# Four kinds of GpSimd products issued in pieces of 256 columns, in a two-block transformer kernel

## The chip, the cores and the metric

The kernel runs on 1 core of one Trainium2 chip. The metric is the device time of one execution in microseconds (us). Three runs of the kernel before took 1583.03, 1586.16 and 1586.99 us; their median, 1586.16 us, is the time before.

The names used below: PE is TensorE's matrix multiply, PEld its weight loads, DVE is VectorE, ACT is ScalarE, POOL is GpSimd, SP is SyncE, which issues the transfers.

## The reference, cut to what matters

Two layers of a first network (a pooling mixer, then stick-breaking attention, each followed by a gated addition) and two of a second one (latent attention, then differential attention, each with a layer norm) run on 512 tokens of 1024 features; the second network has 256 context tokens beside them.

```
h = rms_norm(x, a_norm);  x = x + pool_mixer(h, ...)           # layer 0
A[t,s] = beta[t,s] * prod_{s<j<t} (1 - beta[t,j])              # layer 1, stick-breaking
x = x + (o * silu(z)) @ b_w_out
x = x + (p[i] @ ple_w[i]) * sigmoid(x @ ple_gate_w[i])         # after each of both
x = layer_norm(ALPHA * x + gate * (o @ out_w[i]), ln_g, ln_b)  # second network, twice
```

Every weight matrix of the projections is multiplied with three fp32r products: a float32 number is split into a high part (rounded to fp32r) and a low part (the rest), and high·high, high·low and low·high are added.

## The kernel before, in words

The class `Block` writes the whole program: `layer0`, `layer1`, `mla`, `diff` (`build`, L1485). Activations lie with features or tokens on 128 partitions, 512 columns wide as a rule. A framework turns the calls into one list per engine and sets a semaphore wait wherever an instruction reads or overwrites what another wrote; regions of a tile are told apart, so that two instructions on different columns of one tile do not wait for each other.

**Weights.** `plan` lists units of up to 128x1024 numbers. `w()` hands out unit i and calls `w_advance` (L110): the transfer of unit i + 2 into one of three raw buffers, then the split of unit i + 1: ACT casts raw to the high part `wh` (L126), and L127 subtracts it from raw, which gives the low part `wl`. The first three units and two at the end have L127 on DVE, the other 159 on POOL. `fm` (L151) takes a unit as eight row blocks of 128 columns, `tm` (L157) as four of 256 columns; both walk through the row blocks in order, so the low part's columns are used from left to right, by the second or third product of each row block (L148, L149).

**Other POOL work of the four kinds.** `silu_mul` (L222) multiplies the gate of stick-breaking attention with its sigmoid (L225, 8 times 128x512). In `layer0`, `done` adds squares into `ssacc` (L500, 7 times 128x512). In `stick_steps` (L661), a step has three segments of 512, 384 and 128 columns, or two of 256: ACT makes sigmoid(-l) and sigmoid(l) (L707, L708), DVE scans each segment (L712, a product that runs backwards), POOL multiplies the weights `sb_b` with the scanned `sb_k`, one column further (L715: one instruction of 1023 columns, or two of 255), and PE transposes the result two steps later (`aT_p`, L172), from where ACT and DVE copy it (L731, L733).

**What POOL does besides, unchanged:** normalizing softmax rows (L1055, L1425), head norms (L528), rotary sums (L1000, L1353), and some sums of the layer norm (L818, L1163, L1179, L1180).

**The order of the work.** Each engine runs its list in order. `pipeline` (L254) sets the order inside the attention stages; elsewhere a list scheduler of the framework interleaves the calls.

DVE's part beside it: in the pooling mixer, sums over windows (L446, L449, L451), gates (L461, L463, L471), and the first product's scaling (L441), which frees a PSUM bank; in the layer norm of the second network, L1140 and L1141 (output rows), the small steps of `rsqrt` (L199 to L204), L1151, L1189 (which frees PSUM after the transposes `hT_p`) and the low parts of activations (L234).

Of the kernel before, what the change touches and what calls it, by code (L numbers as in the profile page):

```python
# [10 lines left out]
F32 = mybir.dt.float32  # L11
# [3 lines left out]
ALU = mybir.AluOpType  # L15
# [26 lines left out]
class Block:  # L42
# [67 lines left out]
    def w_advance(self, upto_dma, upto_split):  # L110
        nc = self.nc
        while self.w_dma < min(upto_dma, len(self.wq)):
            u = self.wq[self.w_dma]
            u["raw"] = self.wp.tile([P, 1024], F32, tag="wraw", name="wraw", bufs=3)
            for dst, src in u["src"](self._w_view(u["raw"], u["shape"])):
                nc.sync.dma_start(out=dst, in_=src)
            self.w_dma += 1
        while self.w_split < min(upto_split, len(self.wq)):
            i = self.w_split
            u = self.wq[i]  # L120
            n = math.prod(u["shape"])
            raw = u.pop("raw")
            pool, tag, size, bufs = u["own"] or ("weights", "", 1024, 4)
            h = self.pools[pool].tile([P, size], F32R, tag=tag + "wh", name="wh", bufs=bufs)
            l = self.pools[pool].tile([P, size], F32R, tag=tag + "wl", name="wl", bufs=bufs)
            nc.scalar.copy(h[:, :n], raw[:, :n])  # L126
            (nc.vector if i < 3 or pool == "ow3" else nc.gpsimd).tensor_tensor(out=l[:, :n], in0=raw[:, :n], in1=h[:, :n].bitcast(F32), op=ALU.subtract)  # L127
            u["hl"] = (self._w_view(h, u["shape"]), self._w_view(l, u["shape"]))
            self.w_split += 1

    def w(self):
        i = self.w_next
        self.w_next += 1
        self.w_advance(i + 3, i + 2)
        return self.wq[i].pop("hl")

    def w_cols(self, W, c0, n, own=None):
        return (lambda v: [(v, W[:, c0:c0 + n].rearrange("(k p) n -> p k n", p=P))], (W.shape[0] // P, n), own)
# [83 lines left out]
    def silu_mul(self, out, sg, z):  # L222

        self.nc.scalar.activation(sg, z, AF.Sigmoid)
        self.nc.gpsimd.tensor_tensor(out=out, in0=sg, in1=z, op=ALU.mult)  # L225

    def split(self, x, pool, tag, gain=None, n=512, bufs=8):

# [139 lines left out]
    def layer0(self):  # L368
        nc, a = self.nc, self.a
# [16 lines left out]
        for hf in range(2):  # L386
            for t in range(NT):
                cs = slice(hf * 512, hf * 512 + 512)
# [31 lines left out]
        pool = self.open("mix")  # L420
# [12 lines left out]
        for g, w in enumerate(POOL_WINDOWS):  # L433
# [32 lines left out]
            for j in range(2):  # L466
                c = 2 * g + j
# [7 lines left out]
        pool = self.open("ple0")  # L475
# [9 lines left out]
        pool = self.open("ple0b")  # L485
# [3 lines left out]
        ssacc = self.ssacc = self.sq_acc = xp.tile([P, 512], F32, name="ssacc")  # L489

        def done(c):
            x = xT[:, c, :]
            self.kv_acts.append(self.split(x, "kv", "kv", gain=self.v("kv_norm", c)))
            nc.sync.dma_start(out=self.xf[c], in_=x)
            if c == 0:
                nc.scalar.activation(ssacc, x, AF.Square)
            else:
                sq = pool.tile([P, 512], F32, tag="t2", name="sqc", bufs=4)
                nc.scalar.activation(sq, x, AF.Square)
                nc.gpsimd.tensor_tensor(out=ssacc, in0=ssacc, in1=sq, op=ALU.add)  # L500
            self.b_acts.append(self.split(x, "b", "b", gain=self.v("b_norm", c)))

        self.plan(self.l1_units())
# [157 lines left out]
    def stick_steps(self, c, ks, qs, vtok, ogs, pool):  # L661
# [31 lines left out]
        def first(n, segs):  # L693
            if n == 0 and c == 0:
                prep()
            Q, QL, K = h["Q"], h["QL"], h["K"]
            L = self.p_lg("sb_l")
            for e, i, o in segs:
                w = (i + 1) * P
                qi = slice(i * P, (i + 1) * P)  # L700
                nc.tensor.matmul(L[:, o:o + w], lhsT=Q[e][:, qi], rhs=K[e][:, :w], start=True, stop=False)
                nc.tensor.matmul(L[:, o:o + w], lhsT=QL[e][:, qi], rhs=K[e][:, :w], start=False, stop=False)
                nc.tensor.matmul(L[:, o + i * P:o + w], lhsT=self.identb, rhs=self.maskb, start=False, stop=True)
            kp = pool.tile([P, 1024], F32, tag="sb_k", name="sb_k", bufs=2)
            bt = h["bt", n] = pool.tile([P, 1024], F32, tag="sb_b", name="sb_b", bufs=4)
            vw = (lambda t: t) if len(segs) == 3 else (lambda t: t.rearrange("p (a b) -> p a b", b=512)[:, :, :256])
            nc.scalar.activation(vw(kp), vw(L), AF.Sigmoid, scale=-1.0)  # L707
            nc.scalar.activation(vw(bt), vw(L), AF.Sigmoid)  # L708
            for e, i, o in segs:
                w = (i + 1) * P  # L710
                rev = slice(o + w - 1, o - 1 if o else None, -1)
                nc.vector.tensor_tensor_scan(out=kp[:, rev], data0=kp[:, rev], data1=kp[:, rev], initial=1.0, op0=ALU.mult, op1=ALU.min)  # L712

            for o, w in ((0, 1024),) if len(segs) == 3 else ((0, 256), (512, 256)):
                nc.gpsimd.tensor_tensor(out=bt[:, o:o + w - 1], in0=bt[:, o:o + w - 1], in1=kp[:, o + 1:o + w], op=ALU.mult)  # L715
            if n == 1 and "next" in h:
                h["next"]()

# [800 lines left out]
```

## Time and profile before

| | |
|---|---|
| median of three runs | 1586.16 us |
| the profiled execution, its own time | 1584.99 us |
| its span, first to last instruction | 1583.2 us |
| PE busy / DVE busy / ACT busy / POOL busy | 1488.9 / 925.2 / 733.7 / 603.4 us |
| mean granted TensorE clock | 0.984 of full speed |

Busy times of engines overlap each other. A busy PE is not PE at its peak, because matmuls are pipelined and their ends are modelled. The time of an instruction that is held up by something other than a semaphore (a port that another engine has, for instance) counts as busy; the time before an instruction, while its semaphore is not there, counts as idle and is put down to the instruction that released it. An idle engine that is not the bottleneck costs nothing.

### The profile page before, as it was taken

The numbers are of one execution on the slowest core, as the hardware profiler recorded it, in microseconds if no ns is written. First come the engines' busy times: TensorE is split into PE (matmuls) and PEld (weight loads), VectorE is DVE, ScalarE is ACT, GpSimd is POOL, SyncE is SP. The second block draws the span as 40 slices with busy tenths as digits, with TensorE's granted clock in tenths as the row PEclk, the third lists the DMA queues.
The fourth block names the chain that finished last, engine by engine and source line by source line (L and its number), as shares of the span: only waits on it lengthen the run. The fifth ranks groups of instructions, "written<-read, shape, count | busy, mean of one in ns | idle before, by whom it ended". The sixth has DMA issues, their size and how long they took to land.

```text
span 1583.2 us, 24444 instructions
## 1 busy us (share of the span) xinstructions
PE 1488.9 (94%) x9590; PEld 1247.9 (79%) x9590; DVE 925.2 (58%) x1769; ACT 733.7 (46%) x1347; POOL 603.4 (38%) x431
## 2 busy tenths in 40 slices
PE   6999999999899899999999999997897999999997
PEld 4777889998555578888876667577797989999987
DVE  6676465532776656442465665547857655555576
ACT  5323344435666433332565555533335553555642
POOL 2533555643544453222333332444342424343310
PEclk9999999999999999999999999999899999999999
DMA  5323432323344334311103030434321112121122
GB/s 168 90 77 93 127 119 75 101 87 98 102 134 134 106 120 124 90 44 50 51 1 116 9 120 2 146 120 164 117 81 44 41 41 68 41 66 43 54 77 97
DMA packets 149747, 136.01 MB, mean 86 GB/s; under 512 B 12612, under 2 KB 135224, under 8 KB 149632
## 3 DMA queue, kind: packets, MB, share of 16 engines
q1 hardware_dynamic: 149632, 134.45, 27.4%
q8 instruction: 76, 1.25, 0.3%
q14 instruction: 39, 0.32, 0.1%
HBM read 126.02 MB, written 8.40 MB: 85 GB/s over the span
## 4 chain that ended last, share of the span: by engine, by line
PE 40%; DVE 7%; ACT 5%; issue 3%; DMA 2%; POOL 1%; SPq 0%; DVEq 0%; POOLq 0%; ACTq 0%
PE PT_p L172 4%; PE pv L1076 3%; PE qkv_p L147 2%; PE qkv_p L149 2%; PE qkv_p L148 2%; PE pv L1440 2%; PE gt_p L147 2%; PE gt_p L148 2%; PE gt_p L149 2%; PE lg L147 2%; PE lg L148 1%; ACT pe L1095 1%; PE lg L149 1%; DVE st L1094 1%; PE ada_p L787 1%
## 5 line engine op out<-in xcount | busy, mean ns | idle before, releaser
L127 POOL TENSOR_TENSOR wl<-wraw,wh 128x1024 fp32r<-128x1024 f32 (+2 forms) x159 | 377.0, 2380 | 377.9 <-ACT wh L126 364.8
L126 ACT CAST wh<-wraw 128x1024 fp32r<-128x1024 f32 (+2 forms) x164 | 166.3, 1020 | 282.1 <-issue 60.7
L1095 ACT ACTIVATE pe<-lg,st 128x768 f32<-128x768 f32 x160 | 130.5, 817 | 71.6 <-DVE st L1094 55.4
L1094 DVE TENSOR_REDUCE st<-lg 128x1 f32<-128x768 f32 x160 | 133.5, 843 | 38.8 <-PE lg L1421 20.1
L1055 POOL TENSOR_SCALAR pe<-pe,st 128x768 f32<-128x768 f32 (+1 forms) x96 | 73.4, 768 | 145.8 <-DVE st L1096 130.1
L147 PE MATMUL qkv_p<-wh,h 128*128 128x256 f32 x384 | 109.5, 285 | 0.9 <-ACT V L1366 0.7
L172 PE MATMUL PT_p<-ident,pe 128*128 128x128 f32 x640 | 99.6, 279 | 9.5 <-DVE pe L1426 3.3
L149 PE MATMUL qkv_p<-wh,h 128*128 128x256 f32 x384 | 108.1, 282 | 0.2 <-DVE h L234 0.2
L148 PE MATMUL qkv_p<-wl,h 128*128 128x256 f32 x384 | 108.1, 282 | 0.0
L172 PEld LDWEIGHTS PT_p<-ident,pe 128*128 128x128 f32 x640 | 72.6, 141 | 39.9 <-issue 16.9
L1425 POOL TENSOR_SCALAR pe<-pe,st 128x768 f32<-128x768 f32 x32 | 29.2, 912 | 126.7 <-DVE st L1424 85.5
L147 PE MATMUL out_p<-wh,o 128*128 128x256 f32 x256 | 74.5, 292 | 0.9 <-DVE y L1292 0.8
L147 PEld LDWEIGHTS qkv_p<-wh,h 128*128 128x128 f32 x384 | 72.5, 189 | 3.4 <-ACT V L1366 1.3
L148 PE MATMUL out_p<-wl,o 128*128 128x256 f32 x256 | 73.7, 290 | 1.4 <-POOL wl L127 1.4
L149 PE MATMUL out_p<-wh,o 128*128 128x256 f32 x256 | 73.5, 291 | 0.1
L147 PE MATMUL kv_p<-wh,kv 128*128 128x256 f32 x256 | 72.2, 282 | 1.2 <-ACT kv L236 1.2
L149 PEld LDWEIGHTS qkv_p<-wh,h 128*128 128x128 f32 x384 | 72.4, 189 | 0.4 <-DVE h L234 0.4
L148 PEld LDWEIGHTS qkv_p<-wl,h 128*128 128x128 f32 x384 | 72.6, 189 | 0.0
L148 PE MATMUL kv_p<-wl,kv 128*128 128x256 f32 x256 | 71.6, 280 | 0.0
L715 POOL TENSOR_TENSOR sb_b<-sb_b,sb_k 128x1023 f32<-128x1023 f32 (+1 forms) x32 | 43.0, 1355 | 74.2 <-DVE sb_k L712 44.9
L149 PE MATMUL kv_p<-wh,kv 128*128 128x256 f32 x256 | 71.2, 280 | 0.0
L712 DVE TENSOR_TENSOR_SCAN sb_k<-sb_k 128x512 f32<-128x512 f32 (+3 forms) x64 | 61.2, 996 | 10.4 <-ACT sb_k L707 10.3
(456 smaller groups left out, 4545.6 us busy)
## 6 DMA issues: line engine op xcount, KB each, us to landing
araw<-in_ada_w_dram SPq DMA_DIRECT2D x48, 512.0 KB
wraw<-in_diff_w_in_dram SPq DMA_DIRECT2D x32, 512.0 KB
wraw<-in_out_w_dram SPq DMA_DIRECT2D x24, 512.0 KB
wraw<-in_a_w_in_dram SPq DMA_DIRECT2D x16, 512.0 KB
wraw<-in_ple_gate_w_dram SPq DMA_DIRECT2D x16, 512.0 KB
wraw<-in_w_kv_dram SPq DMA_DIRECT2D x16, 512.0 KB
wraw<-in_b_w_in_dram SPq DMA_DIRECT2D x16, 512.0 KB
wraw<-in_mla_w_in_dram SPq DMA_DIRECT2D x11, 512.0 KB
```

Of the source, the lines that this page charges most:

```text
L126: nc.scalar.copy(h[:, :n], raw[:, :n])
L127: (nc.vector if i < 3 or pool == "ow3" else nc.gpsimd).tensor_tensor(out=l[:, :n], in0=raw[:, :n], in1=h[:, :n].bitcast(F32), op=ALU.subtract)
L147: mm(out, lhsT=lh, rhs=rh, start=start, stop=False)
L148: mm(out, lhsT=lh, rhs=rl, start=False, stop=False)
L149: mm(out, lhsT=ll, rhs=rh, start=False, stop=stop)
L172: self.nc.tensor.transpose(out, in_, self.ident[:in_.shape[0], :in_.shape[0]])
L712: nc.vector.tensor_tensor_scan(out=kp[:, rev], data0=kp[:, rev], data1=kp[:, rev], initial=1.0, op0=ALU.mult, op1=ALU.min)
L715: nc.gpsimd.tensor_tensor(out=bt[:, o:o + w - 1], in0=bt[:, o:o + w - 1], in1=kp[:, o + 1:o + w], op=ALU.mult)
L1055: nc.gpsimd.tensor_scalar(out=pe, in0=pe, scalar1=st[:, 1:2], scalar2=0.0, op0=ALU.mult, op1=ALU.add)
L1076: return nc.tensor.matmul(pv[64 * ee:64 * ee + 64, :], lhsT=V[:, k0 + k, vs], rhs=HH[px][:, k, :], start=(k == 0), stop=(k == nk - 1))
L1094: nc.vector.tensor_reduce(out=st[:, 0:1], in_=L, axis=AX.X, op=ALU.max, negate=True)
L1095: nc.scalar.activation(pe, L, AF.Exp, bias=st[:, 0:1], accum_out=st[:, 2:3])
```

## The change: the four kinds in pieces of 256 columns

A helper `pool_tt` issues a product of two tiles in pieces of 256 columns. L127 (where it is on POOL), L225, L500 and L715 go through it. No other line changes; what is computed is the same, element by element.

```diff
             nc.scalar.copy(h[:, :n], raw[:, :n])
-            (nc.vector if i < 3 or pool == "ow3" else nc.gpsimd).tensor_tensor(out=l[:, :n], in0=raw[:, :n], in1=h[:, :n].bitcast(F32), op=ALU.subtract)
+            if i < 3 or pool == "ow3":
+                nc.vector.tensor_tensor(out=l[:, :n], in0=raw[:, :n], in1=h[:, :n].bitcast(F32), op=ALU.subtract)
+            else:
+                self.pool_tt(l[:, :n], raw[:, :n], h[:, :n].bitcast(F32), ALU.subtract)
...
+    def pool_tt(self, out, in0, in1, op):
+
+        for c in range(0, out.shape[1], 256):
+            cs = slice(c, min(c + 256, out.shape[1]))
+            self.nc.gpsimd.tensor_tensor(out=out[:, cs], in0=in0[:, cs], in1=in1[:, cs], op=op)
...
-        self.nc.gpsimd.tensor_tensor(out=out, in0=sg, in1=z, op=ALU.mult)
+        self.pool_tt(out, sg, z, ALU.mult)
...
-                nc.gpsimd.tensor_tensor(out=ssacc, in0=ssacc, in1=sq, op=ALU.add)
+                self.pool_tt(ssacc, ssacc, sq, ALU.add)
...
-                nc.gpsimd.tensor_tensor(out=bt[:, o:o + w - 1], in0=bt[:, o:o + w - 1], in1=kp[:, o + 1:o + w], op=ALU.mult)
+                self.pool_tt(bt[:, o:o + w - 1], bt[:, o:o + w - 1], kp[:, o + 1:o + w], ALU.mult)
```

On POOL 206 instructions become 724: of L127 146 of 1024 columns, 4 of 768 and 9 of 512 become 614 of 256; of L715 16 of 1023 become 64, and 16 of 255 stay; of L225 and L500 15 of 512 become 30. The lists of DVE, ACT and SP keep their order row for row; PE's moves two tiny products of `ss1` by one row. What changes is POOL's list and who waits for what. In the changed file lines stand 3 to 12 further down; the helper's instruction is L144.

POOL in stick-breaking attention, before: two gates, two weight units and two steps' products (L715; 1023 columns for three segments, 255 for the two short ones). The brackets name the engines whose semaphores the instruction waits for.

```order
L715 TENSOR_TENSOR sb_b<-sb_b,sb_k 128x1023 [waits PE_49,DVE_49,Activation_49,Pool_49]
L225 TENSOR_TENSOR og<-sz,og 128x512 [waits Activation_49]
L127 TENSOR_TENSOR wl<-wraw,wh 128x1024 [waits DMAHW5_49,Activation_49]
L127 TENSOR_TENSOR wl<-wraw,wh 128x1024 [waits DMAHW0_49,Activation_49]
L715 TENSOR_TENSOR sb_b<-sb_b,sb_k 128x1023 [waits PE_49,DVE_49,Activation_49,Pool_49]
```

The same place in the changed kernel:

```order
L144 TENSOR_TENSOR sb_b<-sb_b,sb_k 128x255 [waits DVE_49]
L144 TENSOR_TENSOR og<-sz,og 128x256 [waits Activation_49]
L144 TENSOR_TENSOR og<-sz,og 128x256
L144 TENSOR_TENSOR wl<-wraw,wh 128x256 [waits DMAHW5_49,Activation_49]
L144 TENSOR_TENSOR wl<-wraw,wh 128x256 x3
L144 TENSOR_TENSOR wl<-wraw,wh 128x256 [waits DMAHW0_49,Activation_49]
L144 TENSOR_TENSOR wl<-wraw,wh 128x256 x3
L144 TENSOR_TENSOR sb_b<-sb_b,sb_k 128x256 [waits DVE_49,PE_49,Activation_49]
L144 TENSOR_TENSOR sb_b<-sb_b,sb_k 128x256 [waits DVE_49]
L144 TENSOR_TENSOR sb_b<-sb_b,sb_k 128x256
```

The pieces of a tile stand one behind the other where the tile stood. The first piece of a product waits for the first segment's scan, the second and the fourth for the next ones.

PE in the layer norm of the second network, before: four row blocks of a weight unit (L147 to L149; `out_p<-wl` takes the low part) with transposes of the next activations (`hT_p`) between them.

```order
L147 MATMUL out_p<-wh,o 128x256 [waits Activation_49]
L148 MATMUL out_p<-wl,o 128x256 [waits Pool_49]
L149 MATMUL out_p<-wh,o 128x256
L147 MATMUL out_p<-wh,o 128x256
L148 MATMUL out_p<-wl,o 128x256
L149 MATMUL out_p<-wh,o 128x256
L147 MATMUL out_p<-wh,o 128x256
L148 MATMUL out_p<-wl,o 128x256
```

The same place in the changed kernel:

```order
L156 MATMUL out_p<-wh,o 128x256 [waits Activation_49]
L157 MATMUL out_p<-wl,o 128x256 [waits Pool_49]
L158 MATMUL out_p<-wh,o 128x256
L156 MATMUL out_p<-wh,o 128x256
L157 MATMUL out_p<-wl,o 128x256 [waits Pool_49]
L158 MATMUL out_p<-wh,o 128x256
L156 MATMUL out_p<-wh,o 128x256
L157 MATMUL out_p<-wl,o 128x256 [waits Pool_49]
```

PE's products stand as they did; each row block now waits for its own quarter of the low part, the first one no longer for the whole tile.

## Rows read from the trace of the kernel before

**Rows 1.** Page, part 1: busy us, share of the span, instructions of each engine.

```profile
PE 1488.9 (94%) x9590; PEld 1247.9 (79%) x9590; DVE 925.2 (58%) x1769; ACT 733.7 (46%) x1347; POOL 603.4 (38%) x431
```

**Rows 2.** Busy us by stretch: length, PE, PEld, DVE, ACT, POOL, clock, DMA share, GB/s.

```profile
28.00:140.00 112.00, 99.77 (x413) 78.23 (x412) 82.29 (x95) 33.32 (x45) 49.77 (x27) 0.97 0.32 95
140.00:380.00 240.00, 238.05 (x1602) 217.26 (x1602) 108.78 (x170) 98.44 (x168) 124.79 (x64) 1.00 0.31 98
380.00:535.00 155.00, 141.04 (x809) 89.37 (x808) 112.59 (x164) 99.94 (x143) 73.92 (x48) 0.97 0.35 113
1050.00:1160.00 110.00, 92.26 (x715) 90.32 (x713) 79.83 (x170) 33.23 (x62) 51.32 (x23) 0.92 0.45 149
```

**Rows 3.** Waits of PE, whole span: us in total, times, longest us.

```profile
PE hT_p L172 <- DVE hm L1189: 12.3, 4, 5.8
PE u_p L147 <- DVE u L441: 5.9, 2, 4.3
PE z_p L147 <- DVE zr L461: 3.9, 2, 2.6
...
PE qT_p L172 <- DVE aT L733: 3.7, 1, 3.7
...
PE mix_p L147 <- DVE zr L471: 1.9, 2, 0.9
...
PE out_p L148 <- POOL wl L127: 1.4, 1, 1.4
```

**Rows 4.** Timeline, DVE then POOL, from 1101 us: start us, us, instruction, count.

```profile
1101.75 2.31 DVE L202 TENSOR_TENSOR rs_t<-rs_y,rs_m 128x1 f32<-128x1 f32 x1 [0.98 <-ACT rs_y L201]
1104.10 2.26 DVE L203 SCALAR_TENSOR_TENSOR rs_t<-rs_t,rs_y 128x1 f32<-128x1 f32 x1
1106.29 0.15 DVE L202 TENSOR_TENSOR rs_t<-rs_y,rs_m 128x1 f32<-128x1 f32 x1
...
1101.69 4.65 POOL L127 TENSOR_TENSOR wl<-wraw,wh 128x1024 fp32r<-128x1024 f32 x2 [4.14 <-ACT wh L126]
```

**Rows 5.** DVE groups by form: count | busy us, mean ns of one | idle us before.

```profile
L1141 DVE SCALAR_TENSOR_TENSOR y<-r,y 128x256 f32<-128x256 f32 x24 | 24.8, 1060 | 0.0
...
L463 DVE TENSOR_TENSOR sz<-sz,zr 128x512 f32<-128x512 f32 x8 | 17.1, 2143 | 4.4 <-ACT sz L462 4.4
...
L1140 DVE TENSOR_TENSOR y<-out_p,gate 128x256 f32<-128x256 f32 x24 | 9.2, 415 | 18.5 <-POOL gate L818 13.8 <-PE out_p L149 4.6
```

**Rows 6.** POOL groups by form.

```profile
L127 POOL TENSOR_TENSOR wl<-wraw,wh 128x1024 fp32r<-128x1024 f32 x146 | 357.3, 2456 | 331.4 <-ACT wh L126 324.9 <-issue 3.2 <-PE k_p L172 3.0
...
L715 POOL TENSOR_TENSOR sb_b<-sb_b,sb_k 128x1023 f32<-128x1023 f32 x16 | 32.4, 2022 | 60.1 <-DVE sb_k L712 43.5 <-ACT Q L687 8.3 <-PE aT_p L172 3.5
...
L1353 POOL TENSOR_TENSOR qr<-qr,rt 128x256 f32<-128x256 f32 x12 | 8.8, 738 | 7.2 <-DVE rt L1352 7.2
```

**Rows 7.** Timeline of the mixer's start, DVE, POOL, then PE.

```profile
28.93 2.94 DVE L446 TENSOR_TENSOR win<-u 128x527 f32<-128x527 f32 x1
31.91 1.64 DVE L449 SCALAR_TENSOR_TENSOR pl<-win,u 128x512 f32<-128x512 f32 x1
33.47 2.29 DVE L451 TENSOR_TENSOR hd<-win,invc 128x2 f32<-128x2 f32 x1
35.68 0.68 DVE L441 TENSOR_TENSOR u<-u_p,R 128x512 f32<-128x512 f32 x1
...
28.92 6.83 POOL L127 TENSOR_TENSOR wl<-wraw,wh 128x1024 fp32r<-128x1024 f32 x3 [3.34 <-ACT wh L126]
...
36.42 0.80 PE L147 MATMUL u_p<-h,wh 128*128 128x512 f32 x1 [4.32 <-DVE u L441]
```

**Rows 8.** Timeline of the layer norm, DVE.

```profile
1115.01 5.22 DVE L234 TENSOR_TENSOR hc<-hm,hc 128x256 fp32r<-128x256 f32 x3
```

**Rows 9.** Timeline of stick-breaking attention, DVE then POOL.

```profile
423.21 4.67 DVE L712 TENSOR_TENSOR_SCAN sb_k<-sb_k 128x256 f32<-128x256 f32 x2
...
419.53 5.47 POOL L127 TENSOR_TENSOR wl<-wraw,wh 128x1024 fp32r<-128x1024 f32 x2
424.96 3.95 POOL L715 TENSOR_TENSOR sb_b<-sb_b,sb_k 128x1023 f32<-128x1023 f32 x3
```

## The prediction

> **What bounds the kernel now.** I read the page first. PE is busy for 94% of the span, POOL for 38% [rows 1]: POOL is no bound by its sum, and what the change can give or take has to pass through a wait of PE. So I went to the stretches next. From 140 to 380 us PE is busy for 238 of 240 us; nothing that DVE or POOL does better there can shorten it. PE is short of work in the pooling mixer (12.2 of 112 us idle from 28 us), in stick-breaking attention (14.0 of 155 us from 380) and in the layer norm between the second network's layers (17.7 of 110 us from 1050) [rows 2]. Then PE's waits: the long ones there are for DVE, and all of them end when DVE has freed a PSUM bank: hT_p 12.3 us, u_p 5.9, z_p 3.9, qT_p 3.7, mix_p 1.9. One wait for POOL's low parts is of that size, 1.4 us [rows 3].
>
> Why DVE is late stands in the timeline. At 1101.75 a product of single columns on DVE takes 2.31 us, the next one 2.26, and the same operation at 1106.29 takes 0.15. POOL runs two splits of 1024 columns from 1101.69 to 1106.34, and each of the two DVE operations ends when one of them ends [rows 4]. So DVE is shut out while POOL's instruction runs, gets in behind it, and the following one is shut out by the next. It shows wherever DVE reads two tiles of SBUF: L1141 takes 1.060 us on average for 256 columns, while L1140, which reads one operand from PSUM, takes 0.415; L463 takes 2.143 us for 512 columns [rows 5], where the PSUM form L441 takes 0.68 [rows 7]. The unit of this hold is POOL's instruction, and that is what the change makes shorter.
>
> **POOL's own time.** POOL issues 724 instructions in place of 206. The nearest row to a piece is L1353: two SBUF inputs, 256 columns, 0.738 us. Four of them are 2.95 us against 2.456 for the whole tile [rows 6], so +0.5 us for each of 146 tiles: 73 us. The 16 products of L715 cost between +0.5 (the same rate) and 4 x 0.738 - 2.022 = +0.93: I take 8 us. The 28 instructions of 512 and 768 columns are shorter, so each adds less than 0.5: under 14 us. POOL grows by 81 to 102 us, to about 690, still 44% of the span, and most of it fills time in which it waited for ACT's casts (324.9 us before these splits [rows 6]).
>
> The Trainium skill has another price: GPSIMD Engine Reference, section on performance versus the Vector engine, gives 4497 ns for 2048 columns with two inputs, and a dispatch of tens of cycles. By that an estimate for four pieces is 2.25 us and a little, POOL would hardly grow, and I would say 1577 where I say 1578; L1353's 0.738 us contradicts it for short pieces, and no row shows one of these pieces itself.
>
> **The hold on DVE.** The first hold was 2.31 - 0.15 = 2.16 us, POOL's instruction less about 0.2. For a piece I take 0.738 less the same, about 0.6 (ends: 0.5 and 0.74). A DVE operation that meets a split then waits 0.6 us and no longer up to 2.2. But the next one that reads two tiles meets the next piece. A dense chain of such operations pays four times 0.6, that is the old 2.2; only a chain that has fewer of them than POOL has pieces gains.
>
> *Mixer.* From 28.92 POOL runs three splits, and DVE's chain in front of u is win 2.94, pl 1.64, hd 2.29 us. At 0.7, 0.7 and 0.15 they were held 2.2, 0.9 and 2.1 us; three holds of at most 0.6 are 1.8. u ends 3.4 us sooner, and PE's 4.32 us wait for it shrinks by as much [rows 7]. The second u wait lies behind a dense chain: 0. L463 stands in front of the operations that free z_p and mix_p: 2.14 - 0.68 = 1.46 held becomes 0.6, 0.9 for each of four waits; I take 3 of their 5.8 us. Together 6.4.
>
> *Layer norm.* The longest wait for hm, 5.8 us, lies behind the chain of [rows 4]: seven operations that need the port follow each other there, 7 x 0.6 = 4.2 against 2.16 + 2.11: nothing. The three low parts at 1115.01 take 5.22 us [rows 8]; at 0.41 + 0.6 each they take 3.0: 2.2 less in front of the next hm. Another of these waits lies behind held L1141 rows: I take 2. The low-part wait of 1.4 us goes, because the first row block needs 0.74 us of POOL and not 2.46. With 5.6 worked out I count 5.
>
> *Stick-breaking.* qT_p's 3.7 us wait for a copy behind two scans, 4.67 us for both, held by a split and a product [rows 9]. Two holds of 0.6 would bring the copy some 3 us forward. But the same stretch has POOL at work without a pause, 5.47 us of splits and 3.95 of products, and PE needs those products next. They end later by 2 x 0.5 for the splits, 0.5 for the product, and by the scans that now get in between pieces: 2 to 4 us. PE would find them missing where it now finds the copy missing. I take 1.
>
> *Clock.* It stood at 0.97, 0.97 and 0.92 of 2.4 GHz in these stretches [rows 2]: with 1.2 GHz as the other level, 6.7, 9.3 and 17.6 us were at the lower one, and it fell after PE had been idle (rows 7 lie just ahead of one such fall). Each microsecond that is not at 1.2 GHz gives back at most a half. The ceiling is 16.8 us; as the shorter waits should spare about a fifth of it, 3.
>
> *Costs on the path.* Every product or normalization queued on POOL behind a split starts 0.5 us later for it, and raw buffers come free later for the next transfer. PE's 250 or so waits for POOL become more than 600, one for each piece, but they are waits for work that is mostly done. I take 2 us, with 0 and 10 as ends. In the stretches where PE is full I cost the change at nothing: PE's own backlog hides it, and if that cover went, the price would be the same 0.5 us for each split.
>
> Sum: 6.4 + 5 + 1 + 3 - 2 = 13.4 us. These are shortened waits, each taken alone. When one goes, PE comes sooner to the next unit of weights, whose cast and split it may find unready; I let 60% arrive: 8 us. The profiled execution took 1585.0 us, 1.2 below the median of the runs, so 1577 beside it and **1578** beside the median.
>
> **Rivals.** *More arrives.* If the clock does not fall at all behind the shortened waits and they count in full, 10.4 + 10 = 20 us less: 1566. For it: each fall follows a wait that the change shortens. Against it: the longest, 5.8 us, does not shrink by my working.
>
> *The hold is only divided.* DVE's chains are dense, so that each operation meets a piece and the sum of the holds stays. What is left is the first u wait and the low-part wait, against 2 to 5 us of costs: 1582 to 1588. For it: the working for [rows 4], where seven operations eat the gain.
>
> *POOL late, slower.* In stick-breaking attention POOL is in the loop: scan, product, transposes. There 9 splits and 16 long products grow by 0.5 or more, 12 us or more of POOL work, and scans between the pieces add 0.4 to 0.7 each. It decides where a product's last piece ends after PE has reached its transposes. With 0.5 us late in each of the 16 long products, and 2 us at four places with splits, 16 us; less the mixer's 6: 1596. Against it: PE's only long wait for POOL is a split's [rows 3].
>
> The Trainium skill's page SBUF — State Buffer, section on who interferes with whom, says that the port goes to whichever of the two starts first, for its whole instruction, and that the other blocks. [Rows 4] agree for DVE's side; by the other side POOL can now be blocked at each of four pieces instead of once, which is the second half of this rival.
>
> *It does not do what it says.* If POOL kept the port through queued pieces, DVE would be shut out for 2.95 us a tile and not 2.2: some 5 us slower. Against it: between the two back-to-back splits of [rows 4] a DVE operation got in.
>
> **How the numbers follow.** A measurement of this kernel can tell about 0.3% from no change: 4.8 us, so 1581.4 and 1590.9 are the bounds. Forecast, 5 to 14 us less: 0.50. More arrives: 0.13. Only divided: 0.25, nearly all within the bounds. POOL late: 0.09. Port kept: 0.03, within or just beyond. Faster 0.63, within 0.28, slower 0.09. The range 1566 to 1588 takes in the forecast, the first rival to its value and the second, and leaves out the third and the tails, 2 in 10.
>
> **What would show it.** DVE busy should fall by some 40 to 90 us, with L1141 and L463 near 0.7 and 1.3 us; POOL busy should rise to about 690, a piece taking 0.65 to 0.75 us. PE's u_p wait of 4.3 us should be under 1.5, and the stretch from 28 to 140 us some 5 us shorter; the wait for low parts at out_p should be gone. hT_p's longest wait should stay. If DVE busy does not fall, the hold is not by instruction. If PE waits at aT_p for POOL's products, the third rival holds; if DVE's busy time falls and the stretches keep their length, the second.

## The result and the profile after

| | before | change |
|---|---|---|
| median us (lowest to highest of 4 runs each) | 1585.2 (1583.03 to 1586.99) | 1569.64 (1568.74 to 1570.64) |
| ratio to before | | 0.9897, 95% interval 0.9878 to 0.9915 |
| profiled execution, its span | 1583.2 | 1567.0 |

The ratio, by which all kernels are compared here, is 16.3 us less, 13.5 to 19.3 by its interval (the two medians lie 15.6 us apart). The forecast was 8 us (1578), half of it. The time lies inside the range of the prediction, 1566 to 1588, near the rival "more arrives" at 1566. So the direction held and the size was off by a factor of two.

Page of the changed kernel, part 1, the line that answers to [rows 1]:

```profile
PE 1487.6 (95%) x9590; PEld 1246.6 (80%) x9590; DVE 869.7 (56%) x1769; ACT 733.8 (47%) x1347; POOL 726.1 (46%) x949
```

DVE is busy for 55.5 us less with the same 1769 instructions: that is the hold. POOL is busy for 122.7 us more. Busy time by stretch, columns as in [rows 2], in the changed kernel:

```profile
28.00:140.00 112.00, 103.30 (x444) 81.36 (x443) 76.67 (x98) 37.07 (x52) 71.11 (x85) 1.00 0.33 97
140.00:380.00 240.00, 238.88 (x1594) 217.40 (x1592) 90.61 (x171) 99.32 (x169) 152.62 (x192) 0.99 0.32 98
380.00:535.00 155.00, 140.36 (x822) 89.15 (x822) 111.45 (x167) 99.27 (x141) 99.27 (x131) 0.99 0.35 111
1050.00:1160.00 110.00, 99.56 (x762) 96.29 (x761) 75.44 (x180) 35.98 (x68) 68.56 (x72) 0.92 0.43 144
```

PE does 31 products more in the mixer's 112 us, 13 more in stick-breaking attention's 155 and 47 more in the layer norm's 110 than before. The granted clock rose from 0.97 to 1.00 in the first of these stretches and from 0.97 to 0.99 in the second. PE's waits in the changed kernel, to be laid beside [rows 3]:

```profile
PE aT_p L181 <- DVE aT L742: 5.8, 10, 1.8
...
PE hT_p L181 <- DVE hm L1198: 3.8, 3, 3.1
...
PE out_p L157 <- POOL wl L144: 2.7, 5, 1.0
PE u_p L156 <- DVE u L450: 2.6, 2, 1.3
...
PE mix_p L156 <- DVE zr L480: 2.5, 2, 2.3
PE pT_p L181 <- DMA p_tok<-in_p_dram: 2.5, 1, 2.5
...
PE hT_p L181 <- DVE rs_m L208: 1.8, 1, 1.8
...
PE qT_p L181 <- DVE aT L742: 1.3, 1, 1.3
...
PE z_p L156 <- DVE zr L470: 1.0, 1, 1.0
```

Four waits for DVE shrank: hT_p by 8.5 us (1.8 of it stands under another releaser now), u_p by 3.3, z_p by 2.9, qT_p by 2.4. Others grew: a wait of 2.5 us for the transfer of p_tok is new, low parts cost 1.3 more, mix_p 0.6 more.

### The profile page after: what moved, and what is told of

It reads as the page before. It is cut to its first block, busy times and chain, and to the rows that moved or that the text cites. A ratio compares the mean times of both kernels' runs of the same rounds, so it can differ in the third digit from the quotient of the medians.

```text
span 1567.0 us, 25046 instructions
## 1 busy us (share of the span) xinstructions
PE 1487.6 (95%) x9590; PEld 1246.6 (80%) x9590; DVE 869.7 (56%) x1769; ACT 733.8 (47%) x1347; POOL 726.1 (46%) x949
## 4 chain that ended last, share of the span: by engine, by line
PE 41%; DVE 5%; ACT 4%; POOL 3%; issue 3%; DMA 2%; POOLq 0%; DVEq 0%; SPq 0%; ACTq 0%
PE PT_p L181 4%; PE pv L1085 3%; PE qkv_p L156 3%; PE qkv_p L158 3%; PE qkv_p L157 3%; POOL wl L144 2%; PE gt_p L156 2%; PE gt_p L157 2%; PE gt_p L158 2%; PE pv L1449 2%; PE lg L156 2%; PE lg L157 1%; DVE st L1103 1%; PE lg L158 1%; ACT pe L1104 1%
## 5 line engine op out<-in xcount | busy, mean ns | idle before, releaser
L144 POOL TENSOR_TENSOR wl<-wraw,wh 128x256 fp32r<-128x256 f32 x614 | 476.4, 810 | 315.5 <-ACT wh L126 303.3
L144 POOL TENSOR_TENSOR sb_b<-sb_b,sb_k 128x256 f32<-128x256 f32 (+1 forms) x80 | 59.4, 768 | 46.5 <-ACT sb_b L717 23.5
```

Of the source, the lines that this page charges most:

```text
L144: self.nc.gpsimd.tensor_tensor(out=out[:, cs], in0=in0[:, cs], in1=in1[:, cs], op=op)
```

## Where the time came from

**The mixer.** Timeline of the changed kernel, DVE, POOL and PE (the wait in brackets), to be laid beside [rows 7]:

```profile
30.07 1.28 DVE L455 TENSOR_TENSOR win<-u 128x527 f32<-128x527 f32 x1
31.39 1.11 DVE L458 SCALAR_TENSOR_TENSOR pl<-win,u 128x512 f32<-128x512 f32 x1
32.43 0.67 DVE L460 TENSOR_TENSOR hd<-win,invc 128x2 f32<-128x2 f32 x1
33.02 0.68 DVE L450 TENSOR_TENSOR u<-u_p,R 128x512 f32<-128x512 f32 x1
...
30.05 6.72 POOL L144 TENSOR_TENSOR wl<-wraw,wh 128x256 fp32r<-128x256 f32 x7 [3.34 <-ACT wh L126]
...
33.76 0.51 PE L156 MATMUL u_p<-h,wh 128*128 128x512 f32 x1 [1.32 <-DVE u L450]
```

This is the prediction's working, row for row: the three operations in front of u took 6.87 us and now take 3.06, each held once by one piece, and PE's wait fell from 4.32 to 1.32 us. POOL's line is one run of seven pieces.

**Stick-breaking attention.** PE's qT_p before; then the two scans in front of it and qT_p in the changed kernel; and then the granted clock of 22 us around that place, before and after (columns as in [rows 2]):

```profile
428.12 1.12 PE L172 MATMUL qT_p<-ident,qtok 128*128 128x128 f32 x4 [3.74 <-DVE aT L733]
```

```profile
418.95 2.23 DVE L721 TENSOR_TENSOR_SCAN sb_k<-sb_k 128x256 f32<-128x256 f32 x2
...
421.42 0.66 PE L181 MATMUL qT_p<-ident,qtok 128*128 128x128 f32 x4 [1.26 <-DVE aT L742]
```

```profile
418.00:440.00 22.00, 17.51 (x97) 12.54 (x93) 15.34 (x19) 9.30 (x14) 10.91 (x6) 0.84 0.19 63
```

```profile
411.50:433.50 22.00, 20.73 (x134) 13.64 (x133) 16.12 (x26) 14.01 (x20) 16.08 (x21) 1.00 0.31 98
```

The scans took 4.67 us before [rows 9] and take 2.23. The wait is 2.5 us shorter, and behind it the clock no longer falls: 0.84 of 22 us is 7.0 us at 1.2 GHz, worth up to 3.5 us. Together up to 6 us at a place for which the prediction took 1 us and a share of 3.

The clock at this place goes with the wait in every trace. In the 22 us from the wait's end it is 0.86 to 0.92 in the four kernels that keep a wait of 3.7 us (the kernel before and three of the experiments), and 1.00 in the fourteen traces in which the wait is 1.7 us or less.

**The layer norm.** The changed kernel's chain that answers to [rows 4], DVE and then PE:

```profile
1094.10 0.69 DVE L211 TENSOR_TENSOR rs_t<-rs_y,rs_m 128x1 f32<-128x1 f32 x1 [1.25 <-ACT rs_y L210]
1094.82 0.65 DVE L212 SCALAR_TENSOR_TENSOR rs_t<-rs_t,rs_y 128x1 f32<-128x1 f32 x1
1095.40 0.14 DVE L211 TENSOR_TENSOR rs_t<-rs_y,rs_m 128x1 f32<-128x1 f32 x1
1095.51 0.65 DVE L213 SCALAR_TENSOR_TENSOR rs_y<-rs_t,rs_y 128x1 f32<-128x1 f32 x1
1096.08 0.15 DVE L212 SCALAR_TENSOR_TENSOR rs_t<-rs_t,rs_y 128x1 f32<-128x1 f32 x1
...
1098.47 0.69 PE L181 MATMUL hT_p<-ident,y 128*128 128x128 f32 x2 [3.13 <-DVE hm L1198]
```

A hold is 0.69 - 0.15 = 0.54 us, as estimated (0.6), but it doesn't meet every operation: two of these five took 0.14 and 0.15. The wait that was to stay fell from 5.8 to 3.1 us. The stretch's last wait of hT_p, before and then after:

```profile
1134.46 2.47 DVE L1141 SCALAR_TENSOR_TENSOR y<-r,y 128x256 f32<-128x256 f32 x1
...
1140.29 0.69 PE L172 MATMUL hT_p<-ident,y 128*128 128x128 f32 x2 [3.59 <-DVE hm L1189]
```

```profile
1122.79 0.50 DVE L1150 SCALAR_TENSOR_TENSOR y<-r,y 128x256 f32<-128x256 f32 x1
...
1127.01 0.44 PE L181 MATMUL hT_p<-ident,y 128*128 128x128 f32 x2 [0.33 <-DVE hm L1198]
```

It is all but gone. PE reaches this place 13.3 us sooner than before, 6.7 us of which it had at qT_p (428.12 against 421.42). The longest wait is less sure: in a second trace of the changed kernel it is 3.8 us, not 3.1.

**What came back.** At the mixer's end, before and then after:

```profile
133.91 0.50 PE L147 MATMUL z_p<-plhl,wh 128*128 128x512 f32 x1 [2.58 <-DVE zr L461]
...
140.76 0.38 PE L172 MATMUL pT_p<-ident,p_tok 128*128 128x128 f32 x2
```

```profile
126.67 0.50 PE L156 MATMUL z_p<-plhl,wh 128*128 128x512 f32 x1
...
136.18 0.41 PE L181 MATMUL pT_p<-ident,p_tok 128*128 128x128 f32 x2 [2.49 <-DMA p_tok<-in_p_dram]
```

PE leaves the mixer's products 7.2 us sooner, meets rows that have not landed, and is 4.6 us ahead behind them. At 400 us 3.3 are left: the clock stood at 1.00 from 140 to 380 us before and stands at 0.99 now.

## The experiments

The theory: DVE is shut out for the length of POOL's instruction; shorter instructions shorten holds; and the prediction's error is in its terms for single stages or in the 40% that it took off. Rivals: PE gains because it finds the first quarter of a low part sooner; the products' pieces make the gain; late POOL work eats it. Times are against the kernel before, run beside each kernel; "less" means faster, with 95% intervals. Line numbers in rows are those of the kernel that the rows come from. Each kernel has 4 to 12 runs and one trace; the changed kernel and the version with all three edits have two.

### Splits alone, products alone

The first kernel undoes the pieces of gates, squares and stick-breaking weights, the second those of the splits:

```diff
-                self.pool_tt(bt[:, o:o + w - 1], bt[:, o:o + w - 1], kp[:, o + 1:o + w], ALU.mult)
+                nc.gpsimd.tensor_tensor(out=bt[:, o:o + w - 1], in0=bt[:, o:o + w - 1], in1=kp[:, o + 1:o + w], op=ALU.mult)
...
```

> Only the weights' splits (L127) go in quarters; gates, squares and the weights of stick-breaking attention stay whole. Hold theory (the gain is DVE being shut out for shorter, by the length of POOL's instruction, and the shortened waits of PE arrive in full): nearly all splits, so 12 to 16 us under before, with the mixer and the layer norm as in the changed kernel and at most 3 us lost in stick-breaking attention. Rival (the gain in stick-breaking attention comes from the weights' product in pieces): 10 to 12 us under before, stick-breaking attention as long as before.

> The other half: gates, squares and stick-breaking weights in quarters, the splits whole. Hold theory: 0 to 3 us under before, only between 380 and 535 us, since 62 added pieces are all there is; the other stretches within 0.3 us. POOL-late rival: 0 to 5 us over before, with PE's waits for the transposed products longer.

Measured: splits alone 0.9884 (0.9870 to 0.9897), 18.4 us less, above the 12 to 16 expected; products alone 0.9987 (0.9978 to 0.9996), 2.1 us less. The splits make the gain, and the products' 63 extra pieces add nothing that can be told from zero on top of them. Slower, as the POOL-late rival had it, the products in pieces are not. But they remove the wait at qT_p too, and the clock holds behind it (1.00 over 22 us):

```profile
429.93 0.66 PE L181 MATMUL qT_p<-ident,qtok 128*128 128x128 f32 x4 [0.74 <-DVE aT L742]
```

Two instructions held the scans there, a split and a product [rows 9]; pieces of either one are enough for this wait. Why only 2.1 us come of it here is not shown.

### The four pieces from last to first

```diff
-        for c in range(0, out.shape[1], 256):
+        cols = range(0, out.shape[1], 256)
+        for c in (reversed(cols) if back else cols):
```

with `back` set for the splits alone.

> As the changed kernel, but the four pieces of a split are issued from the last columns to the first, so that PE's first row block has to wait for the whole tile as it did before. Hold theory: DVE busy as in the changed kernel (870 us) and 12 to 16 us under before; PE's waits for low parts cost 1 to 3 us more. Rival (the gain is that PE finds the first quarter of a low part sooner): 0 to 6 us under before, though DVE busy falls as much.

Measured: 0.9894 (0.9881 to 0.9908), 16.8 us less, a little over the first expectation, DVE busy as in the changed kernel (870.3 us against 869.7).

PE's first row block now needs the piece that is issued last. In the trace PE waits for low parts at out_p for as long as in the changed kernel (2.7 us) and once more at z_p for 1.9, and nothing is lost in the time that can be told. The finer waits of PE are not the gain; the rival falls.

### Halves and eighths

```diff
-        for c in range(0, out.shape[1], 256):
-            cs = slice(c, min(c + 256, out.shape[1]))
+        for c in range(0, out.shape[1], 512):
+            cs = slice(c, min(c + 512, out.shape[1]))
```

and the same with 128.

> Pieces of 512 columns instead of 256. A piece of 512 took 1.28 us before, a whole tile 2.4, a quarter 0.74. Hold theory, the gain going with the hold's length: hold of 1.1 us against 2.2 and 0.55, so two thirds of the gain of quarters, 8 to 12 us under before; DVE busy about 885 us. Rival (a dense chain pays the same in any pieces, only the count of free gaps matters): 3 to 7 us under before, DVE busy above 895.

> Pieces of 128 columns. From 512 (1.28 us) and 256 (0.74 us) a piece of 128 should take some 0.47 us, a tile 3.7 us instead of 2.95 and 2.4, and POOL should be busy for some 830 us. Hold theory, the gain going with the hold's length: 17 to 22 us under before. Rival (halves gave as much as quarters, because what a shorter hold gives beyond them is paid back by POOL's longer tiles): 8 to 14 us under before, less than quarters, with longer waits of PE for POOL's low parts and products.

Measured: halves 0.9886 (0.9872 to 0.9899), 18.1 us less, more than either expectation, though DVE was busy for 886.9 us as the first had it; eighths 0.9977 (0.9960 to 0.9995), 3.6 us less, below either expectation, though DVE was busy for only 844.7 us. POOL's groups of the splits in the changed kernel, in halves and in eighths:

```profile
L144 POOL TENSOR_TENSOR wl<-wraw,wh 128x256 fp32r<-128x256 f32 x614 | 476.4, 810 | 315.5 <-ACT wh L126 303.3
```

```profile
L144 POOL TENSOR_TENSOR wl<-wraw,wh 128x512 fp32r<-128x512 f32 x305 | 412.5, 1377 | 358.0 <-ACT wh L126 337.8 <-PE z_p L157 6.9 <-PE kv_p L157 6.3
```

```profile
L144 POOL TENSOR_TENSOR wl<-wraw,wh 128x128 fp32r<-128x128 f32 x1228 | 592.0, 519 | 251.2 <-ACT wh L126 241.2 <-PE kv_p L157 4.6 <-PE k_p L181 3.0
```

A tile of 1024 columns is 2.456 us whole [rows 6], 2 x 1.377 = 2.75 in halves, 4 x 0.810 = 3.24 in quarters, 8 x 0.519 = 4.15 in eighths. With eighths a second thing happens, here in DVE, POOL and PE behind the mixer (the trace is of the slowest of the twelve runs, 4.5 us above their median):

```profile
166.70 8.59 DVE L243 TENSOR_TENSOR x<-xT,x 128x512 fp32r<-128x512 f32 x1 [1.58 <-ACT x L242]
...
157.08 17.66 POOL L144 TENSOR_TENSOR wl<-wraw,wh 128x128 fp32r<-128x128 f32 x40 [4.78 <-ACT wh L126]
...
175.94 0.79 PE L156 MATMUL o_p<-g,wh 128*128 128x512 f32 x1 [5.02 <-DVE xT L491]
```

POOL runs 40 pieces without a pause, each 17.66 / 40 = 0.44 us. A DVE instruction that took 0.84 and 0.85 us just before takes 8.59 and ends with the run: for some 18 pieces it got in between none of them. PE waits 5.0 us in a stretch that was full before. This is the prediction's rival "POOL keeps the port through queued pieces", which was set aside for quarters; it is not true there as a rule (one DVE operation of the changed kernel takes 3.04 us, through some four pieces), and true here.

So the gain goes neither with the hold's length nor with DVE's busy time. Halves show it from the other side: hT_p's waits for hm are 10.2 us, the longest 5.6, hardly less than before (12.3 and 5.8), and yet the time is that of quarters. That a DVE chain's hold in all, against POOL's longer tile, decides is argued here, not shown.

### One stage at a time

Splits go in quarters only while one stage is written, with all products whole:

```diff
+                if self.stage in ('layer0',):
                     self.pool_tt(l[:, :n], raw[:, :n], h[:, :n].bitcast(F32), ALU.subtract)
+                else:
+                    nc.gpsimd.tensor_tensor(out=l[:, :n], in0=raw[:, :n], in1=h[:, :n].bitcast(F32), op=ALU.subtract)
```

> Splits in quarters only while the first network's mixer layer is written, whole in all that follows. If shortened waits arrive at the end in full: the mixer's own 4.5 us (what PE was ahead by when it left the mixer in the changed kernel), so 4 to 6 us under before, DVE busy lower only in the stretch from 28 to 140 us and a little behind it. Rival (a shortened wait is partly given back later, the 60% of the prediction): 1 to 3 us under before.

> Splits in quarters only while the layer norm between the second network's layers is written. If shortened waits arrive in full: 6 to 9 us under before, all of it between 1050 and 1240 us. Rival (60% arrives): 3 to 5 us under before. With the mixer alone and the products alone the sums should then reach 12 to 17 us if the parts add.

> Splits in quarters only while the first network's second layer (stick-breaking attention) is written; splits elsewhere and all products whole. If the prediction's 1 us for this stage was the term that was too small: PE's 3.7 us wait at qT_p goes or falls under 1.5 us, and 3.5 to 6 us are gained, nearly all of it between 420 and 440 us (the products alone gained 2.1 with the splits whole). Rival (the products that come late take the gain back, as the prediction had it): 0 to 2 us under before, with longer waits at aT_p behind the same place.

Measured: the mixer's layer alone 0.9969 (0.9957 to 0.9981), 4.9 us less; the layer norm alone 0.9971 (0.9954 to 0.9988), 4.6 us less; the second layer alone 0.9963 (0.9949 to 0.9976), 5.9 us less. The mixer's 4.9 us are in the range of the first expectation. In its kernel the rows are late too:

```profile
134.93 0.41 PE L184 MATMUL pT_p<-ident,p_tok 128*128 128x128 f32 x2 [2.43 <-DMA p_tok<-in_p_dram]
```

PE is 5.8 us ahead behind that wait (140.76 before). The profiled span ends 5.3 us sooner (1577.9), but the lead is not kept in between. At qT_p, whose wait is as before, 3.6 us are left (428.12 before):

```profile
424.52 1.11 PE L184 MATMUL qT_p<-ident,qtok 128*128 128x128 f32 x4 [3.75 <-DVE aT L745]
```

The clock is 0.89 from 230 to 245 us here, where it was 1.00 in the same 15 us of work before (235 to 250). Near the end it is the other way round: 1.00 over 30 us from 1502, against 0.94 from 1505 before, and that brings the lead from 3.9 back to 5.3. In the second layer's kernel the wait at qT_p has shrunk as expected, and the clock holds (1.00 from 380 to 535 us); PE's timeline there:

```profile
424.04 0.66 PE L184 MATMUL qT_p<-ident,qtok 128*128 128x128 f32 x4 [0.80 <-DVE aT L745]
```

The prediction's 1 us for this stage was too small, and nothing takes the gain back: in this trace PE is 0.2 us ahead at 400 us, 6.3 at 460 and 6.4 at 1050. Of these 6 us 2.9 are the wait. The trace is of the second fastest of ten runs, 1.9 us under their median, and the mean clock of all ten, 0.985, is that of the runs of the kernel before beside them; how much of the 5.9 us is clock stays open. The layer norm's 4.6 us are what its rival expected, not 6 to 9. In its kernel one wait stayed. DVE, POOL and PE there:

```profile
1130.50 2.27 DVE L1153 SCALAR_TENSOR_TENSOR y<-r,y 128x256 f32<-128x256 f32 x1
...
1130.08 4.89 POOL L133 TENSOR_TENSOR wl<-wraw,wh 128x1024 fp32r<-128x1024 f32 x2 [0.24 <-ACT wh L126]
...
1136.12 0.69 PE L184 MATMUL hT_p<-ident,y 128*128 128x128 f32 x2 [3.58 <-DVE hm L1202]
```

The splits beside it already belong to the next stage and are whole here; DVE is held by each of them as before, and PE waits 3.58 us where the changed kernel waits 0.33. So a further kernel has quarters in the layer norm and in the last layer, `('ln', 'diff')`:

> Splits in quarters in the layer norm and in the second network's last layer, whole before; all products whole. If the layer norm's term was too small because its longest wait shrinks and its last one goes: hT_p's wait of 3.6 us is under 1 us, its longest one 3.1, and 7 to 10 us are gained. Rival (the layer norm gives what was predicted, the rest of the gain is elsewhere): 4 to 6 us.

Measured: 0.9957 (0.9938 to 0.9976), 6.8 us less. The time lies between the two expectations, and its interval (3.8 to 9.8 us) takes in both. The trace is of the fastest of twelve runs (1570.90 us, their median 1577.66), 14.2 us under the span before, and says nothing of the size of the gain. In it the layer norm's last wait is 0.54 us and the longest 3.8, not 3.1:

```profile
PE hT_p L184 <- DVE hm L1202: 4.7, 3, 3.8
```

These waits were 12.3 us before [rows 3] and 8.2 in the layer norm's kernel. The parts then sum to 4.9 + 5.9 + 6.8 = 17.6 us, and splits alone measured 18.4: within their intervals the parts add. (Splits in latent attention, between the two, had no run of their own.)

What a single trace can show of a size is seen when the traces are laid side by side, product by product of PE. The table has by how many us PE starts the same product sooner than in the kernel before, at five times of that kernel:

| trace | 160 us | 400 us | 460 us | 1050 us | 1250 us |
|---|---|---|---|---|---|
| changed kernel | 4.5 | 3.3 | 8.4 | 7.1 | 14.2 |
| changed kernel, second trace | 3.0 | 1.1 | 6.2 | 2.6 | 9.8 |
| mixer's layer alone | 5.8 | 3.6 | 3.4 | 3.0 | 3.2 |
| second layer alone | -0.6 | 0.2 | 6.3 | 6.4 | 6.5 |
| layer norm and last layer | 2.3 | 0.9 | 1.9 | 2.8 | 10.9 |
| products alone | -3.1 | -4.9 | -0.1 | -2.5 | -3.0 |
| halves | 3.3 | 4.4 | 10.1 | 10.0 | 15.4 |

The step at qT_p (400 to 460 us) and the one in the layer norm (1050 to 1250) come wherever the splits there are in pieces, 5 to 6 us and 5 to 8. With the products alone in pieces the first step comes too. The lead itself differs between two executions of one kernel by up to 4.5 us (the second trace of the changed kernel is of a run 3.1 us above its median).

### POOL with one input

```diff
-                self.pool_tt(l[:, :n], raw[:, :n], h[:, :n].bitcast(F32), ALU.subtract)
+                for t in (h[:, :n].bitcast(F32), raw[:, :n]):
+                    nc.gpsimd.tensor_scalar(out=l[:, :n], in0=t, scalar1=0.0, scalar2=0.0, op0=ALU.mult, op1=ALU.add)
```

> POOL does no subtraction for the low parts: two passes of one input (multiply by zero) over the whole tile stand in its place, which leaves the low parts of those weights out; the tile takes about as long (two times 1.05 us, as such passes of 1024 columns took before, against 2.4). Everything else is whole as before. Hold theory (DVE is shut out by POOL's two-input instructions, not by POOL being at work): DVE busy falls below quarters, to 800 to 840 us, and the time by 16 to 25 us. Rival (DVE is slowed by any POOL work on the tile): DVE busy above 880 us and under 8 us gained.

Measured: 0.9838 (0.9815 to 0.9860), 25.7 us less, with DVE busy for 860.2 us, between the two expectations. In the layer norm DVE and POOL stand like this:

```profile
1083.08 1.00 DVE L212 TENSOR_TENSOR rs_t<-rs_y,rs_m 128x1 f32<-128x1 f32 x1 [1.25 <-ACT rs_y L211]
...
1083.02 1.04 POOL L131 TENSOR_SCALAR wl<-wh 128x1024 fp32r<-128x1024 f32 x1 [3.28 <-ACT wh L126]
```

So the theory was wrong in one word: POOL's passes of one input hold DVE too, for as long as they last. The pass is short (1.04 us) and the tile no longer than before (two passes, 1.10 and 1.14 us on average). The Trainium skill agrees: SBUF — State Buffer, section on who interferes with whom, has a DVE instruction with two inputs of SBUF contend with any GpSimd instruction that reads SBUF. That quarters would give these 25.7 us too if POOL's tile grew no longer is not shown: this kernel meets no wait for p_tok behind the mixer (PE is 10.6 us ahead there, against 4.5), its low parts are zeros, and it keeps most of hT_p's waits for hm (9.7 us, the longest 4.8).

### Towards a better version

Three edits: lengths by stage (256 in the mixer's layer and the layer norm, 512 elsewhere) with the layer norm's own POOL sums (L1179, L1180) in pieces; the four tiles p_tok in a pool of their own, issued two groups earlier; and both.

```diff
+        n = 256 if self.stage in ('layer0', 'ln') else 512
...
+                tt = self.pool_tt if s == "1" else nc.vector.tensor_tensor
+                tt(out=r, in0=y, in1=lg, op=ALU.mult)
...
+            if g == 2:
+                p_rows = self.p_load(0, ptok)
```

> Quarters in the mixer's layer and in the layer norm, halves (512 columns) elsewhere, and the layer norm's own sums on POOL (L1179, L1180, in the changed kernel L1188 and L1189) in quarters too, which the change leaves whole. If the best length differs by stage (halves were 2 us better in stick-breaking attention, quarters 2 us better in the layer norm): 19 to 23 us under before. The four DVE instructions that take 2.1 to 2.9 us beside those sums in the changed kernel should fall to 0.4 to 1.4 us. Rival (all lengths between 256 and 512 give the same, the sums don't count): 16 to 18 us under before.

> The changed kernel with the transfers of the four tiles p_tok issued two groups earlier, in a place of their own. In the changed kernel PE waits 2.5 us for them right behind the mixer, where before it waited 2.6 us for DVE. If this transfer takes part of the mixer's gain back: that wait goes and 1.5 to 3.5 us more are gained than by the changed kernel, 17 to 20 us under before. Rival (PE finds the next weights late instead, the hidden queue behind the wait): within 1 us of the changed kernel, with another wait of PE between 130 and 145 us.

> The mixed lengths, the layer norm's sums in quarters and the early transfers together. If the three act in different stages and each arrives in full: 21 to 26 us under before. Rival (they overlap): no better than the better of the two alone, 17 to 20 us under before.

Measured: 0.9892 (0.9878 to 0.9905), 0.9896 (0.9881 to 0.9911) and 0.9876 (0.9859 to 0.9892): 17.1, 16.5 and 19.7 us less. By their times all three are what their rivals expected, and each of the first two alone can't be told from the change. The early rows do remove their wait, and PE is 8.2 us ahead of the kernel before at 160 us, against 4.5 in the changed kernel; at 250 us it is 5.4 against 3.4. The clock falls in between. Three stretches (columns as in [rows 2]): with early rows, the changed kernel, and a second trace of the version with all three edits:

```profile
211.00:244.00 33.00, 32.04 (x166) 28.02 (x165) 15.18 (x24) 14.49 (x23) 20.20 (x22) 0.90 0.32 96
```

```profile
211.00:244.00 33.00, 32.03 (x164) 27.19 (x164) 15.81 (x24) 15.32 (x23) 22.69 (x25) 0.95 0.39 120
```

```profile
211.00:244.00 33.00, 32.33 (x190) 28.10 (x190) 16.68 (x31) 15.69 (x26) 20.14 (x18) 1.00 0.32 99
```

At 0.90 the early rows lose 3.3 us there, the changed kernel half of that. But the first trace of the version with all three edits has 0.95 in this stretch, the second 1.00: one kernel, two executions. So this loss is not shown to be the early rows' own. To compare the versions directly, the changed kernel ran once more beside the version with all three edits and one with halves everywhere, products whole, sums in halves and early rows.

> The changed kernel once more, for comparison on one chip with the two versions beside it: 14 to 19 us under before.

> The mixed lengths with the layer norm's sums in quarters and the early rows once more, beside the changed kernel. If what the changed kernel gives back can be had: 3 to 6 us under the changed kernel in this call. Rival (within what a measurement can tell): 0 to 2 us under it.

> Splits in halves everywhere, all products whole, the layer norm's sums in halves, and the early rows. If halves gave as much as quarters because POOL's tiles grow less (2.75 us against 3.2 for 1024 columns in the traces): 3 to 6 us under the changed kernel. Rival (quarters are needed in the mixer and the layer norm, whose chains of DVE are short): as the changed kernel, within 2 us.

| side by side | median us | lowest to highest | ratio to before |
|---|---|---|---|
| changed kernel | 1569.76 | 1568.26 to 1572.88 | 0.9908 (0.9886 to 0.9930) |
| all three edits | 1564.72 | 1561.62 to 1567.27 | 0.9875 (0.9850 to 0.9900) |
| halves everywhere | 1565.54 | 1564.90 to 1566.11 | 0.9879 (0.9856 to 0.9902) |

Each run of both versions is below each run of the changed kernel: 5.0 and 4.2 us by the medians, as the first expectations had it. The two can't be told apart. That halves do as well with fewer instructions speaks for them.

## Why the prediction was off

- **The mechanism was right.** DVE is shut out while POOL's instruction runs, pieces shorten it, DVE busy fell by 55.5 us (40 to 90 forecast). L1141 fell from 1060 to 740 ns on average, L463 from 2143 to 1145 (0.7 and 1.3 us forecast); the rows are these:

```profile
L1150 DVE SCALAR_TENSOR_TENSOR y<-r,y 128x256 f32<-128x256 f32 x24 | 17.1, 740 | 0.0
...
L472 DVE TENSOR_TENSOR sz<-sz,zr 128x512 f32<-128x512 f32 x8 | 9.2, 1145 | 9.8 <-ACT sz L471 9.8
```

- **The mixer's waits were right, its gain a little less.** 6.4 us were forecast for u_p, z_p and mix_p. The waits at u_p and z_p shrank by 6.2, the one at mix_p grew by 0.6, and the stage alone gives 4.9.
- **The first step that failed is the term for stick-breaking attention, "I take 1".** The 3 us by which the copy comes forward were worked out, then set off against products that POOL would deliver late. They are not missed: PE's waits at aT_p are for DVE and went from 5.3 to 5.8 us, and the stage alone gives 5.9. The wait gave 2.5 us, and the clock that no longer falls behind it up to 3.5 more in the trace. The prediction shared 3 us of clock over all stages; the mean granted clock, 0.984 before and 0.987 after, gives (1 - 0.984) x 1583.2 = 25.3 against (1 - 0.987) x 1567.0 = 20.4, so 4.9 us. All four runs of the changed kernel have 0.987 to 0.989.
- **The second is "I let 60% arrive".** It took 5.4 of the 13.4 us that were added up; 16.3 came. It fits the mixer: of the 7.2 us by which PE was ahead at the last z_p, 4.6 were left behind the transfer of p_tok and 3.3 at 400 us. The reason was not the one named, a cast or a split, but a transfer that PE's own lateness had hidden, and the clock. Behind qT_p and the layer norm no such loss is seen where only that stage is in pieces: 6.3 us at 460 us and 6.5 at 1250 in the second layer's kernel, 10.9 at 1250 and 11.3 at 1500 in the one with the layer norm and the last layer. The changed kernel itself loses 1.3 us between 460 and 1050 us in one trace and 3.6 in the other.
- **The layer norm's term was too small, "nothing" above all.** Seven holds of 0.6 us were counted for the longest wait. Of the six single-column operations from 1094 us on four were held, and the wait shrank by 2.7 us (2.0 in the second trace). The last wait, of which 2 us were taken, lost 3.3. 5 us were forecast; 4.6 (with that last wait left in) to 6.8 us were measured with the other stages whole. The clock in the stretch did not change, 0.92 before and after.
- **POOL's price was right for a piece by itself**: the median piece took 0.738 us, the figure of L1353. The mean is 0.810 and POOL's busy time 726 us, not 690, because 114 of the 614 pieces took more than 0.85 us; DVE was at work beside every one of them. The Trainium skill's page GPSIMD Engine Reference (section on performance versus the Vector engine) would have had four pieces in an estimated 2.25 us; they take 3.24, and the row of L1353 was the better guide. The forecast that the low-part wait at out_p goes was wrong: it is five waits of up to 1.0 us, 2.7 us in all.
- **The rival "more arrives"** came nearest, 20 us against 16.3, and for half of its reason: the clock no longer falls behind qT_p, but it still falls in the layer norm. Its ground, that each fall follows a wait that the change shortens, does not hold at 529 us, where the clock fell before behind a wait of 2.4 us at pv; that wait is 2.1 us in the changed kernel, and the clock still falls there.

Not settled: why halves and quarters come out alike in the sum, though halves hardly shorten the layer norm's waits; part of it may be chance, since two traces of the changed kernel differ by 4.5 us at 1050 us. Nor is it settled whether the products' pieces gain anything beside quartered splits.

## What to carry to other kernels

Where GpSimd works beside a VectorE chain that PE waits for, look for VectorE rows of one form with very different durations: the long ones end when a GpSimd instruction ends. Cut the GpSimd instruction in two or four, not finer, since each cut lengthened its tile by 0.24 to 0.30 us here and a queue of very short pieces can shut VectorE out (8.59 us with pieces of 128 columns). Then look at what PE meets sooner, a transfer above all, and price a wait with the clock that falls behind it. Take sizes from many runs, not from one trace of each kernel.

## What the runs showed of the hardware

- VectorE is not sure of a turn between two queued GpSimd instructions. With pieces of 128 columns one VectorE instruction waited through some 18 of them, 8.59 us. The Trainium skill (SBUF — State Buffer, who interferes with whom) gives the port to the first comer for its whole instruction; here it was kept over many instructions. Why sometimes and not as a rule was not tried.
- GpSimd passes with one input hold VectorE as the two-input ones do (1.00 us for single columns beside a pass of 1.04 us).
- TensorE's clock fell to 0.86 to 0.92 of full speed over 22 us behind a PE wait of 3.7 us at one place (qT_p), in all four traces that have this wait, and stayed at 1.00 in all fourteen in which it is 1.7 us or less. At another place, near 240 us, one kernel had 0.95 in one execution and 1.00 in the next.
